# Opening stage of a hybrid decoder layer: inverse root by Ln and Exp, conditioning loads issued three k tiles ahead, two squares added before their sum

## Chip, cores and metric

One core of a Trainium2 chip runs the whole program. The metric is the device time in microseconds (us), the median of several executions. Engines: PE is TensorE (matmuls; PEld its weight loads), DVE is VectorE, ACT is ScalarE, POOL is GpSimd, SP is the sync engine, which issues nearly all DMAs here.

## The reference, cut to what matters

One decoder layer on a sequence of 1024 tokens of width 1024. The change touches only its opening: RMSNorm of x, scaled and shifted by a conditioning vector, and the first columns of the input projection.

```python
c_act = jax.nn.silu(c)
shift, scale, gate = jnp.split(c_act @ ada_w + ada_b, 3, axis=-1)
h = rms_norm(x, norm_g) * (1 + scale[:, None, :]) + shift[:, None, :]
(sq, sk, sv, sz, dq, dk_, dv_, dz, ...) = jnp.split(h @ w_in, offsets, axis=-1)
...   # three token mixers (stick-breaking attention, gated DeltaNet, GLA)
merged = g_sb * (y_sb @ proj_sb) + g_gdn * (y_gdn @ proj_gdn) + g_gla * (y_gla @ proj_gla)
return x + gate[:, None, :] * (merged @ w_out)
```

`rms_norm` is x · 1/sqrt(mean(x²) + 1e-6) · g, with the mean over the 1024 channels of a token.

## The kernel before

The activations lie transposed, channels on the 128 partitions: eight k tiles `xs[k]` of 128 channels by 1024 tokens. Every projection needs h in two parts, `h_hi` (rounded for fast matmuls) and `h_lo` (the remainder), so a product is three matmuls of 128x512 where one would do.

**Order of work.** PE's instructions run in the order in which the program text makes them. On all other engines and in SP's queue a planner reorders: it goes by the order of the text, by its own forecast of when inputs are ready, and it gives out the buffers of one tag in the order of the text. Each queue then runs strictly in the planned order, and waits where an input or a buffer is late.

**The sum of squares (lines 311 to 333).** `square` makes x² of a k tile on POOL, DVE or ACT. `add_up` has PE multiply by a matrix of ones into two PSUM banks, one for each half of the tokens; a float32 matmul of 128x512 is two passes in the trace, so one `add_up` is four passes. There are five: k tiles 0, 1, 2 alone, then 3+4+5 added up, then 6+7. The inverse root is ACT's Sqrt of each half and DVE's reciprocal of each half (line 333). A dummy Sqrt (line 322) is there to have the table of that function loaded early.

**The conditioning (lines 341 to 369).** Each k tile needs two columns of `mod`, shift and scale. For k tiles 0 and 1 `by_product` has PE do it, two tiles of `ada` with 16 matmuls of one column (32 records) each pair. For k tiles 2 to 7 `by_rows` has DVE do it: two loads of 512 KB (line 352) and two reductions over 128x1024 (line 367). The tiles come from the pool `hp` (tag "h", 16 buffers), which also holds the 16 tiles of h.

**The k loop (lines 377 to 420).** For k tile k: `by_rows`; `split` of the raw weights (ACT line 151, DVE line 152); `amp` (line 398); x·amp·rstd on DVE (line 403), `h_hi` on ACT (line 406), `h_lo` on DVE (line 408); then 24 matmuls of 128x512 on PE into eight PSUM banks, in the order h_hi, h_lo, h_hi. The raw weights (line 381 for k up to 2, line 392 for later ones) have three buffers. In the text the ada loads of k tile k (k from 3) stand at the head of its own turn, after the h tiles of the k tiles before it.

**What follows.** The small projections, then head 1's projections as filler between the DeltaNet steps. Eight more reductions of the same kind, for the later `gate` (lines 297 to 301), stand much further down in the text; the planner fits them in where it sees DVE free.

Of the kernel before, what the change touches and what calls it, by code (L numbers as in the profile page):

```python
# [15 lines left out]
AF = mybir.ActivationFunctionType  # L16
# [3 lines left out]
P = 128  # L20
D = 1024
T = 1024
KT = D // P
# [10 lines left out]
O_DQ, O_DK, O_DV, O_DZ = 2048, 2560, 3072, 3584  # L34
# [18 lines left out]
def kernel(ctx: ExitStack, tc: tile.TileContext, xT: bass.AP, c: bass.AP,  # L53
# [3 lines left out]
    nc = tc.nc  # L57
# [15 lines left out]
    def big(tag, w=1024, dt=F32):  # L73
        return mp.tile([P, w], dt, tag=tag, name=tag, bufs=3 if tag == "u5" else 2)
# [4 lines left out]
    def bank(pool, tag, *shape):  # L79
        return pool.tile([P, *shape], F32, tag=tag, name=tag)  # L80
# [12 lines left out]
    def mm(out, lhsT, rhs, cost, **kw):  # L93
        clock[0] += cost
        return nc.tensor.matmul(out, lhsT=lhsT, rhs=rhs, **kw)  # L95
# [17 lines left out]
    def C(name, i=0, n=1):  # L113
        o = COLS[name][0] + i
        return col[:, o:o + n]
# [14 lines left out]
    one_c = ones[:, 0:1]  # L130
    eps_c = cp.tile([P, 1], F32, name="eps_c")
# [9 lines left out]
    c_row = big("u8")  # L141
    for hf in range(2):
        sl = slice(hf * HALF, (hf + 1) * HALF)
# [5 lines left out]
    def split(hi, lo, raw, scale=None):  # L149
        if scale is None:  # L150
            nc.scalar.copy(out=hi, in_=raw)  # L151
            nc.vector.tensor_sub(out=lo, in0=raw, in1=hi.bitcast(F32))  # L152
        else:
            nc.scalar.activation(out=hi, in_=raw, func=AF.Copy, scale=scale)  # L154
            nc.vector.scalar_tensor_tensor(out=lo, in0=raw, scalar=scale, in1=hi.bitcast(F32),  # L155
                                           op0=ALU.mult, op1=ALU.subtract)

    def raw_tile():
        return wp.tile([P, 4, P], F32, tag="raw", name="raw")
# [144 lines left out]
    ms = [bank(pl, "lv", HALF) for _ in range(2)]  # L304
    halves = [slice(hf * HALF, (hf + 1) * HALF) for hf in range(2)]
    root = cp.tile([P, 1], F32, name="root")

    def square(k, out, eng):
        for sl in halves if k == KT - 1 else (slice(0, T),):
            if eng is nc.scalar:  # L310
                eng.activation(out=out[:, sl], in_=xs[k][:, sl], func=AF.Square)
            else:
                eng.tensor_mul(out=out[:, sl], in0=xs[k][:, sl], in1=xs[k][:, sl])
        return out

    def add_up(x2, start=False, stop=False):
        for hf, sl in enumerate(halves):
            mm(ms[hf], ones, x2[:, sl], 858, start=start, stop=stop)

    for k, eng in ((0, nc.gpsimd), (1, nc.vector), (2, nc.scalar)):  # L320
        add_up(square(k, big(("u4", "u4", "u5")[k]), eng), start=(k == 0))
    nc.scalar.activation(out=root, in_=one_c, func=AF.Sqrt)
    part, more = square(3, big("u6"), nc.vector), [big("u6"), big("u5")]
    for k in (4, 5):
        nc.vector.tensor_add(out=part, in0=part, in1=square(k, more[k - 4], nc.scalar))
# [2 lines left out]
    rstd = big("u5")  # L328
    for hf, sl in enumerate(halves):
        nc.vector.tensor_add(out=last[0][:, sl], in0=last[0][:, sl], in1=last[1][:, sl])  # L330
        mm(ms[hf], ones, last[0][:, sl], 858, start=False, stop=True)
        nc.scalar.activation(out=rstd[:, sl], in_=ms[hf], func=AF.Sqrt, scale=1.0 / D, bias=eps_c)
        nc.vector.reciprocal(out=rstd[:, sl], in_=rstd[:, sl])
    na = cp.tile([P, 1], F32, name="na")
    amp = cp.tile([P, KT], F32, name="amp")


    PRE = 2
    first_mod = bank(pt, "tr", HALF)

    def both(ap, k):
# [2 lines left out]
    def conditioning2(k):  # L344
        tiles = [hp.tile([P, T], F32, tag="h", name="ada") for _ in range(2)]
        if k < PRE:
            for i, t in enumerate(tiles):
                nc.sync.dma_start(out=t, in_=adaP[2 * k + i])
            return lambda: by_product(k, tiles)
        for i, t in enumerate(tiles):  # L350
            j = 8 * i + k
            nc.sync.dma_start(out=t, in_=adaT[j * P:(j + 1) * P, :])
        return lambda: by_rows(k, tiles)

    def by_product(k, tiles):
        for i, t in enumerate(tiles):
            at = 2 * k + i
            for kk in range(KT):
                mm(first_mod[:, at:at + 1], t[:, kk * P:(kk + 1) * P], c_col[:, kk:kk + 1], 120,
                   start=(kk == 0), stop=(kk == KT - 1))  # L360
        nc.vector.tensor_add(out=both(mod, k), in0=first_mod[:, 2 * k:2 * k + 2],
                             in1=both(C("ada_b", 0, 24), k))

    def by_rows(k, tiles):
        for i, t in enumerate(tiles):
            j = 8 * i + k
            nc.vector.tensor_tensor_reduce(out=t, in0=t, in1=c_row, scale=1.0, scalar=0.0,
                                           op0=ALU.mult, op1=ALU.add, accum_out=mod[:, j:j + 1])
        nc.vector.tensor_add(out=both(mod, k), in0=both(mod, k), in1=both(C("ada_b", 0, 24), k))
# [3 lines left out]
    f_ps = [[None, None] for _ in first]  # L373
    f_banks = ((pa, "acc"), (pa, "acc"), (pm, "mx"), (pm, "mx"), (pt, "tr"), (pl, "lv"),
               (pl, "lv"), (pl, "lv"))
    raws, conds = [], []
    for k in range(KT):
        conds.append(conditioning2(k))
        raw = raw_tile()
        wsrc = w_in[k * P:(k + 1) * P, O_DQ:O_DQ + 4 * 512].rearrange("p (g n) -> p g n", g=4)  # L380
        nc.sync.dma_start(out=raw, in_=wsrc[:, :, 0:P])
        raws.append(raw)
        if k == 2:
            break
    for k in range(PRE):
        conds[k]()
    for k in range(KT):
        if k >= 3:
            conds.append(conditioning2(k))
            raw = raw_tile()  # L390
            wsrc = w_in[k * P:(k + 1) * P, O_DQ:O_DQ + 4 * 512].rearrange("p (g n) -> p g n", g=4)
            nc.sync.dma_start(out=raw, in_=wsrc[:, :, 0:P])
            raws.append(raw)
        if k >= PRE:
            conds[k]()
        w = wp.tile([P, 2, 4, P], F32R, tag="w", name="w")
        split(w[:, 0], w[:, 1], raws[k])
        nc.vector.scalar_tensor_tensor(out=amp[:, k:k + 1], in0=mod[:, 8 + k:9 + k], scalar=1.0,
                                       in1=C("norm_g", k), op0=ALU.add, op1=ALU.mult)
        hi = hp.tile([P, T], F32R, tag="h", name="h_hi")  # L400
        lo = hp.tile([P, T], F32R, tag="h", name="h_lo")
        for sl in halves if k == 0 else (slice(0, T),):
            nc.vector.scalar_tensor_tensor(out=xs[k][:, sl], in0=xs[k][:, sl],
                                           scalar=amp[:, k:k + 1], in1=rstd[:, sl],
                                           op0=ALU.mult, op1=ALU.mult)
            nc.scalar.activation(out=hi[:, sl], in_=xs[k][:, sl], func=AF.Identity,  # L406
                                 bias=mod[:, k:k + 1])
            nc.vector.scalar_tensor_tensor(out=lo[:, sl], in0=xs[k][:, sl],  # L408
                                           scalar=mod[:, k:k + 1],
                                           in1=hi[:, sl].bitcast(F32),  # L410
                                           op0=ALU.add, op1=ALU.subtract)
        h_hi.append(hi)
        h_lo.append(lo)
        for g in range(4):
            for hf in range(2):
                if k == 0:
                    pool, tag = f_banks[2 * g + hf]
                    f_ps[g][hf] = bank(pool, tag, HALF)
                sl = slice(hf * HALF, (hf + 1) * HALF)
                for n, (a, r) in enumerate(((0, hi), (0, lo), (1, hi))):  # L420
                    mm(f_ps[g][hf], w[:, a, g, :], r[:, sl], 216,
                       start=(k == 0 and n == 0), stop=(k == KT - 1 and n == 2))
# [53 lines left out]
    raw = big("u7").rearrange("p (k n) -> p k n", k=KT)  # L476
    for o, dst, n in ((O_LR, 0, RANK), (O_DB, 32, NH), (O_DA, 64, NH)):
        nc.sync.dma_start(out=raw[:, :, dst:dst + n],
                          in_=w_in[:, o:o + n].rearrange("(k p) n -> p k n", p=P))
# [858 lines left out]
    for n, (h, q) in enumerate(halves):  # L1338
        g, key = G[h], f"{h}.{q}"
# [9 lines left out]
    for n, (h, q) in enumerate(halves):  # L1349
        g, key = L[h], f"{h}.{q}"  # L1350
# [80 lines left out]
```

## Time and profile before

| | us |
|---|---|
| median of 3 runs | 1532.16 |
| lowest and highest run | 1530.81 and 1535.56 |
| the profiled execution | 1534.0 |
| its span | 1532.2 |
| PE busy in the span | 1480.8 (97%) |
| DVE busy | 851.6 (56%) |
| ACT busy | 676.5 (44%) |
| idle of PE before lines waiting on h_hi and h_lo of the k loop | 13.9 and 5.8 |

Busy time of PE is not PE at its peak: the granted clock has two levels, 2.4 GHz (1.00 in the profile) and 1.2 GHz (0.50), and a matmul at the lower one counts as busy for twice as long. The idle time in front of a group of instructions is put down to what ended it. Over the whole span PE is nearly always busy; the views of the first 110 us are what this case is about.

### The profile page before, as it was taken

What the parts mean: (1) busy time and instruction counts of PE and PEld (TensorE: products, weight loads), DVE (VectorE), ACT (ScalarE), POOL (GpSimd) and SP (SyncE); (2) the same over time, 40 slices, a digit from 0 to 9 for tenths busy, and PEclk for the clock granted to TensorE, in tenths of its full rate; (3) what the DMA queues carried; (4) which work ended last, traced back from release to release, by engine and by line L of the source; (5) the groups of instructions that cost most, each with busy time, mean ns of one, the idle gap of its engine ahead of it and who ended that gap; (6) DMA issues with size and microseconds to landing.
All of it is one profiled execution on the core that took longest, in us unless ns stands there. A gap on an engine that the chain in (4) does not pass through costs nothing.

```text
span 1532.2 us, 26643 instructions
## 1 busy us (share of the span) xinstructions
PE 1480.8 (97%) x10632; PEld 1241.6 (81%) x10632; DVE 851.6 (56%) x1839; ACT 676.5 (44%) x1468; POOL 148.6 (10%) x295
## 2 busy tenths in 40 slices
PE   8779999999999999999999999999999999999998
PEld 5658777777878787878878999899988888888887
DVE  5776746656653566757666524553555326474721
ACT  5136846452563646647466623342434442322200
POOL 1001223224230000000000100010000000000000
PEclk7889999999999999999999999999999999999999
DMA  7532423131232111112121212110222334353342
GB/s 253 199 97 55 112 75 88 50 91 43 64 93 71 42 43 52 46 53 60 49 60 29 77 56 62 49 36 27 58 69 83 106 107 124 118 148 117 119 144 76
DMA packets 162470, 126.48 MB, mean 83 GB/s; under 512 B 23429, under 2 KB 139269, under 8 KB 162346
## 3 DMA queue, kind: packets, MB, share of 16 engines
q1 hardware_dynamic: 162202, 124.47, 27.6%
q8 instruction: 83, 1.36, 0.4%
q14 instruction: 41, 0.34, 0.1%
q10 hardware_dynamic: 144, 0.31, 0.1%
HBM read 99.80 MB, written 24.95 MB: 81 GB/s over the span
## 4 chain that ended last, share of the span: by engine, by line
PE 80%; DVE 9%; ACT 3%; issue 3%; DMA 3%; POOL 2%; SPq 0%; POOLq 0%; DVEq 0%; ACTq 0%
PE acc L95 64%; PE lv L95 6%; PE mx L95 6%; PE tr L122 2%; DVE u L431 2%; PE tr L95 1%; DVE w L152 1%; DVE w L616 1%; DVE w L618 1%; POOL c L284 1%; DMA v<-gam_d 1%; DMA raw<-in_w_in 1%; DVE u L1156 0%; DMA xd<-w 0%; POOL w L642 0%
## 5 line engine op out<-in xcount | busy, mean ns | idle before, releaser
L95 PE MATMUL acc<-h_hi,w 128*128 128x512 f32 x1856 | 658.9, 410 | 13.9 <-ACT h_hi L406 13.9
L95 PEld LDWEIGHTS acc<-h_hi,w 128*128 128x128 f32 x1856 | 353.0, 190 | 85.9 <-ACT h_hi L406 16.1
L95 PE MATMUL acc<-h_lo,w 128*128 128x512 f32 x928 | 367.4, 396 | 5.8 <-DVE h_lo L408 5.8
L95 PEld LDWEIGHTS acc<-h_lo,w 128*128 128x128 f32 x928 | 177.1, 191 | 35.6 <-DVE h_lo L408 8.8
L95 PE MATMUL acc<-whi,h_hi 128*128 128x256 f32 x640 | 186.9, 292 | 0.0
L95 PE MATMUL acc<-wlo,h_hi 128*128 128x256 f32 x640 | 180.7, 282 | 0.0
L95 PE MATMUL acc<-whi,h_lo 128*128 128x256 f32 x640 | 180.7, 282 | 0.0
L95 PE MATMUL acc<-u,w 128*128 128x512 f32 x768 | 176.5, 391 | 0.0
L95 PEld LDWEIGHTS acc<-u,w 128*128 128x128 f32 x768 | 144.2, 188 | 31.6
L151 ACT CAST w<-raw 128x512 fp32r<-128x512 f32 x144 | 84.9, 619 | 149.8 <-PE acc L95 90.3
L152 DVE TENSOR_TENSOR w<-raw,w 128x512 fp32r<-128x512 f32 x144 | 97.5, 688 | 56.5 <-ACT w L151 55.8
L95 PEld LDWEIGHTS acc<-whi,h_hi 128*128 128x128 f32 x640 | 122.3, 191 | 1.4 <-issue 0.7
L95 PEld LDWEIGHTS acc<-wlo,h_hi 128*128 128x128 f32 x640 | 122.4, 191 | 0.1
L95 PEld LDWEIGHTS acc<-whi,h_lo 128*128 128x128 f32 x640 | 122.2, 191 | 0.0
L284 POOL TENSOR_TENSOR c<-c,mhalf 128x4 f32<-128x4 f32 (+1 forms) x56 | 55.0, 981 | 582.3 <-DVE c L282 580.9
L95 PE MATMUL acc<-m_hi,w 128*128 128x512 f32 x256 | 79.0, 389 | 0.0
L1156 DVE TENSOR_TENSOR_SCAN u<-u,zero_c 128x128 f32<-128x128 f32 (+7 forms) x32 | 43.4, 1356 | 36.3 <-ACT u L1154 36.3
L155 DVE SCALAR_TENSOR_TENSOR w<-raw,col,w 128x128 fp32r<-128x128 f32 x96 | 29.5, 349 | 55.3 <-ACT w L154 55.3
L95 PEld LDWEIGHTS mx<-r,u 128*128 128x128 f32 x288 | 44.1, 190 | 17.3 <-DVE r L797 4.9
L95 PEld LDWEIGHTS acc<-m_hi,w 128*128 128x128 f32 x256 | 48.0, 188 | 10.0
L95 PE MATMUL mx<-r,u 128*128 128x128 f32 x288 | 48.4, 280 | 5.6 <-POOL u L766 2.2
L95 PE MATMUL lv<-u,u 128*32 128x32 f32 (+5 forms) x528 | 48.9, 250 | 4.0 <-DVE u L699 4.0
(256 smaller groups left out, 2169.1 us busy)
## 6 DMA issues: line engine op xcount, KB each, us to landing
raw<-in_w_in SPq DMA_DIRECT2D x160, 256.0 KB, 3.0
g_dram<-v SPq DMA_DIRECT2D x36, 256.0 KB, 2.2
v<-g_dram SPq DMA_DIRECT2D x36, 256.0 KB, 2.7
u<-in_xT SPq DMA_DIRECT2D x16, 512.0 KB, 5.0
u<-y_dram SPq DMA_DIRECT2D x16, 512.0 KB, 3.7
ada<-in_adaT SPq DMA_DIRECT2D x12, 512.0 KB, 4.5
u<-in_adaT SPq DMA_DIRECT2D x8, 512.0 KB, 4.0
v<-gam_d SPq DMA_DIRECT2D x16, 256.0 KB, 3.3
```

Source lines behind the costliest of these rows:

```text
L95: return nc.tensor.matmul(out, lhsT=lhsT, rhs=rhs, **kw)
L122: nc.tensor.transpose(out=out, in_=in_, identity=ident[:k, :k])
L151: nc.scalar.copy(out=hi, in_=raw)
L152: nc.vector.tensor_sub(out=lo, in0=raw, in1=hi.bitcast(F32))
L155: nc.vector.scalar_tensor_tensor(out=lo, in0=raw, scalar=scale, in1=hi.bitcast(F32), op0=ALU.mult, op1=ALU.subtract)
L284: nc.gpsimd.tensor_tensor(out=out, in0=out, in1=mhalf[:, 0:n], op=ALU.pow)
L431: nc.vector.scalar_tensor_tensor(out=t, in0=r[:, tap:tap + T], scalar=C("conv", j + tap), in1=t, op0=ALU.mult, op1=ALU.add)
L616: nc.vector.tensor_tensor(out=t3, in0=L3[:, w:16, j:w].broadcast_to([32, n, w]), in1=Xl3[:, j:w, 0:w].broadcast_to([32, n, w]), op=ALU.mult)
L618: nc.vector.tensor_sub(out=Xl3[:, w:16, 0:w], in0=Xl3[:, w:16, 0:w], in1=t3)
L1156: nc.vector.tensor_tensor_scan(om[:, 0:n][:, ::-1], om[:, 0:n][:, ::-1], zero_c.broadcast_to([P, n]), 1.0, ALU.mult, ALU.add)
```

## The change

Four edits, all in the opening.

- The squares of k tiles 1 and 2 are added on DVE and go through one `add_up`, and the one of k tile 0 follows: four `add_up`s in place of five.
- The inverse root is Ln of each half on ACT, then one Exp with scale -0.5 over all 1024 tokens. The two reciprocals are gone. The dummy is a Square and an Ln on an element of `c_row`, so that it comes after the Silu that makes `c_row`.
- The loads of k tiles 3 to 7 are asked for three turns earlier: at turn k, behind the h pair of k tile k, first the raw weights and then the ada pair of k tile k+3.
- The order of the first three turns' loads is as it was.

```diff
-    for k, eng in ((0, nc.gpsimd), (1, nc.vector), (2, nc.scalar)):
-        add_up(square(k, big(("u4", "u4", "u5")[k]), eng), start=(k == 0))
-    nc.scalar.activation(out=root, in_=one_c, func=AF.Sqrt)
+    low = [square(k, big(("u4", "u4", "u5")[k]), eng)
+           for k, eng in ((0, nc.gpsimd), (1, nc.vector), (2, nc.scalar))]
+    nc.vector.tensor_add(out=low[1], in0=low[1], in1=low[2])
+    add_up(low[1], start=True)
+    add_up(low[0])
+    nc.scalar.activation(out=root, in_=c_row[:, T - 1:T], func=AF.Square)
+    nc.scalar.activation(out=root, in_=root, func=AF.Ln, bias=one_c)
...
-        nc.scalar.activation(out=rstd[:, sl], in_=ms[hf], func=AF.Sqrt, scale=1.0 / D, bias=eps_c)
-        nc.vector.reciprocal(out=rstd[:, sl], in_=rstd[:, sl])
+        nc.scalar.activation(out=rstd[:, sl], in_=ms[hf], func=AF.Ln, scale=1.0 / D, bias=eps_c)
+    nc.scalar.activation(out=rstd, in_=rstd, func=AF.Exp, scale=-0.5)
...
-    for k in range(KT):
-        conds.append(conditioning2(k))
-        raw = raw_tile()
...
+    AHEAD = 3
...
+    def load_first(k):
         raw = raw_tile()
         wsrc = w_in[k * P:(k + 1) * P, O_DQ:O_DQ + 4 * 512].rearrange("p (g n) -> p g n", g=4)
         nc.sync.dma_start(out=raw, in_=wsrc[:, :, 0:P])
+        return raw
+
+    for k in range(AHEAD):
+        conds.append(conditioning2(k))
+        if k < 3:
+            raws.append(load_first(k))
     for k in range(PRE):
         conds[k]()
     for k in range(KT):
-        if k >= 3:
-            conds.append(conditioning2(k))
...
         if k >= PRE:
             conds[k]()
...
+        if k + 3 < KT:
+            raws.append(load_first(k + 3))
+        if k + AHEAD < KT:
+            conds.append(conditioning2(k + AHEAD))
...
```

## Rows read from the trace of the kernel before

**Rows 1.** Stretches: length, busy PE, PEld, DVE, ACT, POOL, PEclk, DMA share, GB/s

```profile
32.27:42.17 9.90, 9.29 (x24) 6.60 (x25) 9.90 (x17) 2.23 (x3) 0.20 (x2) 0.61 0.31 85
42.17:53.30 11.13, 11.04 (x49) 8.82 (x47) 8.25 (x15) 2.31 (x4) 0.00 (x0) 1.00 0.71 236
64.05:77.30 13.25, 8.41 (x24) 6.05 (x24) 10.09 (x18) 1.76 (x2) 0.00 (x0) 0.74 0.52 178
42.17:108.48 66.31, 49.55 (x170) 37.28 (x168) 45.42 (x78) 14.30 (x21) 2.33 (x2) 0.85 0.51 164
108.48:160.00 51.52, 51.52 (x244) 42.89 (x243) 36.61 (x60) 37.12 (x67) 12.35 (x15) 1.00 0.24 62
```

**Rows 2.** What PE waited for from 43 to 108.5: us, times, longest

```profile
PE acc L95 <- ACT h_hi L406: 11.6, 5, 4.2
PE acc L95 <- DVE h_lo L408: 5.2, 5, 1.5
```

**Rows 3.** The chain of waits, 42 to 109: start, us, what

```profile
79.69 5.64 DMA ada<-in_adaT
```

**Rows 4.** SP's queue in order of time: start, us, line, what it issues

```profile
14.43 1.61 SPq L352 DMA_DIRECT2D ada<-in_adaT  x2
...
43.80 0.39 SPq L392 DMA_DIRECT2D raw<-in_w_in  x1
44.23 0.97 SPq L352 DMA_DIRECT2D ada<-in_adaT  x2
```

**Rows 5.** DVE by group, 22 to 108.5: count, busy us, mean ns, idle before

```profile
L367 DVE CUSTOM_DVE_ANT_0 ada<-ada,u 128x1024 f32<-128x1024 f32 x12 | 14.5, 1221 | 3.1 <-DMA ada<-in_adaT 3.0
L299 DVE CUSTOM_DVE_ANT_0 u<-u,u 128x1024 f32<-128x1024 f32 x8 | 9.8, 1219 | 4.6 <-DMA u<-in_adaT 4.6
L403 DVE SCALAR_TENSOR_TENSOR u<-u,amp,u 128x1024 f32<-128x1024 f32 x7 | 9.0, 1281 | 0.2
L408 DVE SCALAR_TENSOR_TENSOR h_lo<-u,mod,h_hi 128x1024 fp32r<-128x1024 f32 x7 | 9.0, 1280 | 0.6 <-ACT h_hi L406 0.6
L152 DVE TENSOR_TENSOR w<-raw,w 128x512 fp32r<-128x512 f32 x10 | 6.8, 689 | 7.8 <-ACT w L151 7.8
...
L398 DVE SCALAR_TENSOR_TENSOR amp<-mod,col 128x1 f32<-128x1 f32 x8 | 1.2, 156 | 0.2
```

**Rows 6.** PE and PEld in order of time, start of the program

```profile
7.88 11.40 PE L95 MATMUL lv<-u,ones 128*128 128x512 f32 x20 [0.38 <-POOL u L313]
...
9.75 0.34 PEld L95 LDWEIGHTS lv<-u,ones 128*128 128x128 f32 x1 [0.52 <-issue]
...
13.81 0.19 PEld L95 LDWEIGHTS lv<-u,ones 128*128 128x128 f32 x1 [0.24 <-issue]
...
19.12 3.63 PE L95 MATMUL tr<-c_col,ada 128*128 128x1 f32 x32
...
23.00 6.99 PE L95 MATMUL tr<-c_col,ada 128*128 128x1 f32 x32 [0.25 <-DVE mod L361]
```

**Rows 7.** DVE in order of time, start of the program

```profile
10.60 1.22 DVE L313 TENSOR_TENSOR u<-u 128x1024 f32<-128x1024 f32 x1 [1.31 <-DMA u<-in_xT]
12.97 2.56 DVE L325 TENSOR_TENSOR u<-u,u 128x1024 f32<-128x1024 f32 x2 [1.15 <-ACT u L311]
...
23.06 6.56 DVE L333 RECIPROCAL u<-u 128x512 f32<-128x512 f32 x2
...
30.71 1.41 DVE L403 SCALAR_TENSOR_TENSOR u<-u,amp,u 128x512 f32<-128x512 f32 x2
```

**Rows 8.** ACT in order of time, start of the program

```profile
9.33 1.06 ACT L311 ACTIVATE u<-u 128x1024 f32<-128x1024 f32 x1 [1.19 <-DMA u<-in_xT]
...
19.32 0.69 ACT L332 ACTIVATE u<-lv,eps_c 128x512 f32<-128x512 f32 x1 [0.17 <-PE lv L95]
```

**Rows 9.** ACT later on: an Ln and the next Exp, in order of time

```profile
510.16 0.72 ACT L903 ACTIVATE v<-v,ones 128x512 f32<-128x512 f32 x1
...
515.80 1.28 ACT L944 ACT_TABLE_LOAD   x1
```

More of the change, by code (lines that the diff above doesn't have):

```diff
@@ L375 @@
                (pl, "lv"), (pl, "lv"))
-    raws, conds = [], []
-    for k in range(KT):
-        conds.append(conditioning2(k))
+    def load_first(k):
         raw = raw_tile()
@@ L381 @@
         nc.sync.dma_start(out=raw, in_=wsrc[:, :, 0:P])
-        raws.append(raw)
-        if k == 2:
-            break
+        return raw
+    raws, conds = [], []
+    for k in range(AHEAD):
+        conds.append(conditioning2(k))
+        if k < 3:
+            raws.append(load_first(k))
     for k in range(PRE):
@@ L387 @@
     for k in range(KT):
-        if k >= 3:
-            conds.append(conditioning2(k))
-            raw = raw_tile()
-            wsrc = w_in[k * P:(k + 1) * P, O_DQ:O_DQ + 4 * 512].rearrange("p (g n) -> p g n", g=4)
-            nc.sync.dma_start(out=raw, in_=wsrc[:, :, 0:P])
-            raws.append(raw)
         if k >= PRE:
```

## The prediction

> **What bounds the kernel now.** Over the whole span PE is nearly always busy, so a microsecond saved matters where PE stands still or runs at its lower level. I read the stretches first [rows 1]. From 42.17 to 108.48, k tiles 1 to 7 of the opening loop, PE is busy for 49.55 of 66.31 us and the granted clock averages 0.85. Two k tiles in the middle of it, 42.17 to 53.30, show what dense work looks like: 11.04 us busy for 48 matmuls at clock 1.00, so 5.5 us a k tile. A later one, 64.05 to 77.30, takes 13.25 us at clock 0.74: some 5 us of idle, and 8.41 us of busy time for work worth 5.5. Seven dense k tiles would need 7 x 5.5 = 38.5 us; the stretch is 66.31 - 38.5 = 27.8 us longer. Next, what PE waits for there [rows 2]: h_hi 11.6 us and h_lo 5.2, which is all of its 16.8 us of idle. The other 11 us are the lower level after each gap.
>
> Then what makes h late. The chain of waits goes through the landing of an ada pair, 5.64 us at 79.69 [rows 3]. SP's queue says why it is late [rows 4]: the pair of k tile 2 is issued at 14.43, that of k tile 3 only at 44.23, behind a raw load at 43.80. Nothing but its place holds it there. The pool has 16 buffers, six hold ada tiles, and the text asks for k tile 3's pair behind three h pairs. DVE's groups tell the same from the other side [rows 5]: reductions idle 3.0 us for ada, the later gate's reductions, squeezed between, 4.6 us for theirs, and the weight split 7.8 us for ACT. DVE is busy for 45.42 of the 66.31 us [rows 1], so it isn't full.
>
> **The change part by part.**
>
> *Squares.* One DVE add of 1.28 us (two took 2.56) [rows 7] replaces one `add_up`. PE's passes fall from 20 to 16. But PE now begins with the sum of squares 1 and 2. ACT's square of k tile 2 ends at 9.33 + 1.06 = 10.4 [rows 8]; the new dummy adds a table load of 1.28 us after the Silu, half of which falls into ACT's 1.19 us of waiting, so 10.4 to 10.9. With the add: 11.7 to 12.2. If DVE squares k tile 3 first (10.60 to 11.82) it is 13.1 [rows 7]. PE thus starts at 12.2 (11.7 to 13.1) instead of 7.88 [rows 6]. A weight load with its gap came every 0.86 us at 9.75 and every 0.43 us at 13.81 [rows 6]: the two levels. Before, about five of the 11.4 us lay at the lower one. I take five again: 6 passes at 0.86, 10 at 0.43, 9.5 us in all, so the sum ends at 21.7 where it ended at 19.1. Bounds: 11.7 with only three slow passes gives 19.9, 13.1 with sixteen gives 26.9. So this edit costs 2.6 us (0.8 to 7.8). Counting passes alone would have said a gain of 4 x 0.43 = 1.7. The Trainium skill (TensorE: Matmul & The Clock Gate, The HAM clock gate) says that the throttled state is the default and that activity releases it. By that rule taking early work from PE delays its rise; the rows of the 20 passes agree, 0.86 before 0.43.
>
> *by_product.* Its 32 records took 3.63 us at the upper and 6.99 us at the lower level [rows 6]. [...] The first may lose the upper, since the sum ends later; I take 5 us. So mod of k tile 0 is there at 26.7, and the second ends at 26.7 + 0.3 + 7.0 = 34.0 (bounds 19.9 + 2 x 3.63 = 27.2 and 26.9 + 14.3 = 41.2).
>
> *Inverse root.* Two reciprocals of 3.28 us ran until 29.62, and behind them the first x·amp·rstd only at 30.71 [rows 7]. In their place: Ln of the second half 0.69 (as Sqrt at 19.32) [rows 8], a table load 1.28, Exp about 1.1. That the load is needed shows later in this trace: an Ln at 510.16 and, before the next Exp, a load of 1.28 us at 515.80 [rows 9]. rstd is ready at 21.7 + 0.9 + 1.28 + 1.1 = 25.0, before mod at 26.7, so the root leaves the path. DVE then makes h of k tile 0 at 27 to 30 while PE still runs the second by_product, and PE's 2.3 us of waiting at k tile 0 disappear. What is late next is the second by_product itself. k tile 0 runs from 34.0; with half its 24 matmuls at the lower level that is 12 x 0.46 + 12 x 0.23 = 8.3 us, so to 42.3. Before it ran from 32.27 to 42.17 at clock 0.61 [rows 1]. The start therefore comes out even (5 us better, 7 worse).
>
> *Conditioning loads.* Issued behind the h pair of k, the pair of k+3 has about two and a half turns, some 14 us, where landing took 5.64 [rows 3]. Cover gone, 5.64 us a k tile would come back. In front of it on SP stands the raw load of k+3, which waits until the split of k has freed its buffer; that is before h_lo of k, so it doesn't hold the pair up. Behind them the gate loads wait, which are wanted only at the very end. Buffers: k tile 5's pair needs those of k tile 0, free when by_product is over; k tile 7's those of k tile 4. The wait for ada is gone; what is next is DVE's own work. A k tile costs it two reductions 2.44, 1.28 + 1.28, 0.69 and two small operations of 0.16 [rows 5], 6.0 us; without reductions 3.4. From 34.0 (mod of k tile 1; k tile 2's reductions fit in before): 2 x 3.4 + 5 x 6.0 = 36.8, so h_lo of k tile 7 at 70.8. Eight gate reductions at 1.22 + 0.16 add up to 11.0 and run in this stretch now. None inside: 70.8; all inside: 81.8. Half: 76.3. With the last k tile's 5.5 us the loop ends at 76.3, 81.8 or 87.3 by DVE; by PE, 42.3 + 38.5 = 80.8. I take 82. Before: 108.5. Gain 26.5 us.
>
> *What follows.* From 108.48 to 160 PE never waits, and DVE is busy for 36.61 of 51.52 us [rows 1]. Gate reductions pushed out there, four of them 5.5 us, find 15 us of idle, but the chain of waits runs along DVE there. I charge 3.5 us (0 to 6).
>
> **Sum.** 26.5 - 3.5 = 23 us off. The profiled execution took 1534.0 us, 1.8 above the median, which gives 1511 for it; for the median, 1532.16 - 23 = 1509.
>
> **Rivals.**
>
> A, DVE takes the place of the loads. If the planner keeps one gate reduction in each k tile, DVE needs 6.0 + 1.4 = 7.4 us where PE needs 5.5. PE then waits about 2 us each time, and the lower level comes back, as in the row of clock 0.74, where 24 matmuls took 8.41 busy us [rows 1]. Half of that loss back on each of seven k tiles is 1.5 us: 7 x (7.4 + 1.5) = 62, loop end 104, gain 4.5; where the lower level returns in half of them only, 57, loop end 99, gain 9.5. With nothing given back later, the time is 1523 to 1528. Against it: the gate reductions filled DVE's idle time, which is going.
>
> B, the pairs don't come earlier: the planner gives them the same place on SP, behind raw loads whose buffers are late. Then only the start moves, which comes out even: 1530 to 1534. Against it: the second use of the pool's buffers is what held them, and the text now asks three turns earlier.
>
> C, slower: the late sum. If PE stays at the lower level through all sixteen passes and both by_products, k tile 0 starts at 41.2 instead of 32.27, less the 2.3 us no longer waited: up to 7 us more. It decides only where the loop gains less than that, that is where DVE paces k tiles 1 to 7 at 8.5 us or more. Time 1535 to 1539. For it: the passes at 0.86. Against it: DVE's 6.0.
>
> **How the numbers follow.** Main forecast 0.75: loop end 76 to 87 by the number of gate reductions inside, 5 us better or 7 worse by the start, 0 to 6 us given back; taken together, since the ends hardly meet, 1497 to 1521. A 0.13, B 0.06, C 0.06. The range goes to 1525, into A's times, and leaves out the rest of A, B and C, some 0.18. Differences of 0.3% (4.6 us) are about what a measurement of this kernel can tell from no change. Faster by more: the main case and most of A, 0.86; within: 0.08 (B, the rest of A); slower: 0.06.
>
> **What would show it.** After: the sum of squares with 16 passes starting near 12 and ending near 22; no reciprocal, an Exp ending before mod of k tile 0; ada pairs of k tiles 3 and 4 issued by 40; no DVE idle on ada; PE granted 1.00 through k tiles 1 to 7, each about 5.5 to 6 us; the loop's end near 82. Wrong if PE still waits more than 1 us for h_hi at several k tiles, if the small projections' start doesn't move by 20 us, or if PE waits that are new appear between 80 and 180.

## The result, and the profile after

The changed kernel took 1508.49 us (median of four runs, 1507.0 to 1512.01) against 1533.86 for the kernel before on the same chip: a ratio of 0.9838, interval 0.9809 to 0.9866, so 25 us less where 23 were forecast. The profiled execution took 1507.8 us with a span of 1506.0; before it was 1534.0 and 1532.2. All times of the trace below are from that execution.

First the stretches that answer to [rows 1]: start, length, busy PE, PEld, DVE, ACT, POOL, PEclk, DMA share, GB/s.

```profile
24.66:40.03 15.37, 13.35 (x57) 11.47 (x57) 11.67 (x22) 3.72 (x6) 0.20 (x2) 0.67 0.55 174
40.03:78.11 38.08, 38.08 (x170) 31.54 (x168) 35.95 (x61) 14.82 (x22) 1.82 (x1) 1.00 0.61 185
```

The second line is k tiles 1 to 7. They now take 38.08 us with PE busy all through at clock 1.00; in [rows 1] the same seven took 66.31 us, busy for 49.55 of them at clock 0.85. Both parts of the loss went together: the 16.8 us of idle and the 11 us of lower level behind it. DVE is busy for 35.95 of the 38.08 us, so there is little room left on it.

What PE waits for from 25 to 110, answering to [rows 2] (us, times, longest):

```profile
PE acc L95 <- DVE h_lo L409: 1.8, 1, 1.8
PE tr L95 <- DVE mod L366: 0.3, 1, 0.3
```

The wait for h_hi is gone; the one for h_lo that is left lies in k tile 0. SP's queue, answering to [rows 4], gives the reason: the pairs of k tiles 3 to 7 are issued from 27.04 on instead of 44.23 (the last at 53.98 instead of 84.21), the first of them right behind a raw load.

```profile
26.62 0.38 SPq L384 DMA_DIRECT2D raw<-in_w_in  x1
27.04 0.98 SPq L357 DMA_DIRECT2D ada<-in_adaT  x2
...
34.69 1.58 SPq L357 DMA_DIRECT2D ada<-in_adaT  x2
...
43.15 0.92 SPq L357 DMA_DIRECT2D ada<-in_adaT  x2
...
47.26 0.89 SPq L357 DMA_DIRECT2D ada<-in_adaT  x2
...
53.98 0.98 SPq L357 DMA_DIRECT2D ada<-in_adaT  x2
```

The raw loads of k tiles 3 to 7 are no such cause, though the change asks for them earlier too. Before, the planner had them in the queue ahead of the pairs, two at 30.82, then at 38.23, 43.80 and 49.23:

```profile
30.82 2.31 SPq L392 DMA_DIRECT2D raw<-in_w_in  x2
...
38.23 0.39 SPq L392 DMA_DIRECT2D raw<-in_w_in  x1
...
49.23 0.38 SPq L392 DMA_DIRECT2D raw<-in_w_in  x1
```

After, they go out at 26.62, 34.27, 37.16, 42.66 and 48.25. The last three come 1 us earlier, while the pairs come 17 to 32 us earlier. (The raw load at 43.80 in [rows 4] is that of k tile 6, not of k tile 3.)

DVE by group from 22 to 78.1 (count, busy us, mean ns, idle before), answering to [rows 5]: the reductions (line 372 now) wait for no ada tile, the weight split (line 152) not for ACT, and of the later gate's eight reductions (line 299) two lie in the loop instead of all eight.

```profile
L372 DVE CUSTOM_DVE_ANT_0 ada<-ada,u 128x1024 f32<-128x1024 f32 x12 | 14.5, 1219 | 0.0
...
L152 DVE TENSOR_TENSOR w<-raw,w 128x512 fp32r<-128x512 f32 x10 | 6.8, 687 | 0.0
...
L299 DVE CUSTOM_DVE_ANT_0 u<-u,u 128x1024 f32<-128x1024 f32 x2 | 2.4, 1215 | 1.9 <-DMA u<-in_adaT 1.9
```

PE at the start, answering to [rows 6] (start, us, instruction, in brackets the idle time before it and what ended it):

```profile
12.05 9.11 PE L95 MATMUL lv<-u,ones 128*128 128x512 f32 x16 [4.36 <-DVE u L322]
20.99 3.63 PE L95 MATMUL tr<-c_col,ada 128*128 128x1 f32 x32
24.88 5.72 PE L95 MATMUL tr<-c_col,ada 128*128 128x1 f32 x32 [0.25 <-DVE mod L366]
30.46 0.77 PE L95 MATMUL acc<-h_hi,w 128*128 128x512 f32 x1
33.03 0.79 PE L95 MATMUL acc<-h_lo,w 128*128 128x512 f32 x1 [1.80 <-DVE h_lo L409]
```

The sum of squares begins when DVE's add (line 322) is done and has 16 passes. ACT at the start, answering to [rows 8], shows the new root: two Ln, a table load of 1.28 us, one Exp, done at 24.25.

```profile
20.34 0.69 ACT L336 ACTIVATE u<-lv,eps_c 128x512 f32<-128x512 f32 x1 [3.11 <-PE lv L95]
21.20 0.69 ACT L336 ACTIVATE u<-lv,eps_c 128x512 f32<-128x512 f32 x1 [0.17 <-PE lv L95]
21.90 1.28 ACT L337 ACT_TABLE_LOAD   x1
23.19 1.06 ACT L337 ACTIVATE u<-u 128x1024 f32<-128x1024 f32 x1
```

And a wait that the kernel before doesn't have, from the waits of PE from 78 to 130:

```profile
PE tr L122 <- DVE gam_c L541: 4.0, 1, 4.0
```

**The ledger.** The loop ends at 78.1 instead of 108.5, 30.4 us earlier. By the end of the DeltaNet preparation's triangular solve (PE's last wait for DVE's u there) 175.24 stands against 201.72, 26.5 us earlier, and at the end of the span 26.2. So 3.9 of the 30.4 us go in the 97 us behind the loop, and almost nothing after that. The stretch from the loop's end to that point, before and after, with the columns of [rows 1]:

```profile
108.48:201.72 93.24, 86.85 (x523) 70.92 (x522) 67.06 (x176) 68.40 (x121) 23.91 (x42) 0.98 0.31 78
```

```profile
78.11:175.24 97.13, 89.77 (x523) 72.65 (x522) 75.41 (x194) 70.32 (x122) 26.58 (x43) 0.95 0.38 102
```

PE does the same work (523 records of matmuls in both) and stands idle for 7.4 us instead of 6.4: the new wait of 4.0 us makes it late, and it then waits 3.3 us inside the solve where before it waited 6.4. The larger part, 2.9 us, is busy time: the granted clock averages 0.95 instead of 0.98. From the start of the new wait on, 112.83 to 125.16, it is 0.72; before, the same work (142.94 to 155.70) ran at 1.00.

### The profile page after: what moved, and what is told of

The parts are those of the page before. It is cut to its first block, busy times and chain, and to the rows that moved or that the text cites. A ratio compares the mean times of both kernels' runs of the same rounds, so it can differ in the third digit from the quotient of the medians.

```text
span 1506.0 us, 26643 instructions
## 1 busy us (share of the span) xinstructions
PE 1467.5 (97%) x10628; PEld 1235.0 (82%) x10628; DVE 844.5 (56%) x1838; ACT 679.5 (45%) x1471; POOL 150.5 (10%) x295
## 4 chain that ended last, share of the span: by engine, by line
PE 83%; DVE 8%; ACT 3%; DMA 3%; POOL 2%; issue 2%; SPq 0%; POOLq 0%; DVEq 0%; ACTq 0%
PE acc L95 66%; PE lv L95 7%; PE mx L95 6%; PE tr L122 2%; DVE u L436 1%; PE tr L95 1%; DVE w L621 1%; DVE w L623 1%; DVE w L152 1%; POOL w L647 1%; POOL c L284 1%; DMA w<-ad 1%; DMA w<-xd 1%; DVE u L1161 1%; DMA u<-in_xT 0%
## 5 line engine op out<-in xcount | busy, mean ns | idle before, releaser
L155 DVE SCALAR_TENSOR_TENSOR w<-raw,col,w 128x128 fp32r<-128x128 f32 x96 | 29.5, 349 | 55.7 <-ACT w L154 48.9
L95 PE MATMUL lv<-u,u 128*32 128x32 f32 (+5 forms) x528 | 48.9, 251 | 2.6 <-DVE u L704 2.6
```

## The experiments

Each was measured against the kernel before on the same chip; that kernel's medians were 1534.2, 1534.5 and 1534.8 us in the three groups. "Loop end" is PE's end with the 24 matmuls of k tile 7 in the profiled execution. The changed kernel itself was measured in the first and the third group, not in the second, which has the kernels with pairs two ahead, without gate reductions and with the low part first; comparisons of these with it go across groups, which are on different chips. Expectations name the changed kernel, the one before and the theories as they stood then.

### Which edit carries the gain

**The changed kernel again**, for its scatter.

> The changed kernel again, beside the parts of it that follow, so that they can be compared with it on one chip. Both theories expect 24 to 26 us less than before (ratio 0.983 to 0.985).

Measured: 1511.86 us, ratio 0.9852 (0.9837 to 0.9866). Loop end at 81.8 instead of 78.1, and the new wait of 4.0 us is there again. The instructions are the same; PE's first 40 us aren't:

```profile
11.68 10.13 PE L95 MATMUL lv<-u,ones 128*128 128x512 f32 x16 [4.03 <-DVE u L322]
21.65 4.15 PE L95 MATMUL tr<-c_col,ada 128*128 128x1 f32 x32
26.05 6.99 PE L95 MATMUL tr<-c_col,ada 128*128 128x1 f32 x32 [0.25 <-DVE mod L366]
32.90 0.77 PE L95 MATMUL acc<-h_hi,w 128*128 128x512 f32 x1
```

Here the second small product runs at the lower level to its end (6.99 us against 5.72), and k tile 0 with it: from 30 to 42 the granted clock is 0.51. A loop end thus carries 4 us of scatter from one execution to the next.

**The loads alone**, with root and squares as before:

```diff
+    AHEAD = 3
...
-        if k >= 3:
-            conds.append(conditioning2(k))
...
+        if k + 3 < KT:
+            raws.append(load_first(k + 3))
+        if k + AHEAD < KT:
+            conds.append(conditioning2(k + AHEAD))
```

> The loads three turns ahead alone; root and squares as before. Theory (the loads are the gain): the sum of squares ends at 19.1 us and k tile 0 starts near 32.3 as before, k tiles 1 to 7 run on PE's time (38 us, no wait above 1 us), so the loop ends near 81 instead of 108.5, and 3 to 5 us are given back later: 22 to 25 us less, ratio 0.984 to 0.986. Rival (DVE's reciprocals were the brake, the loads merely follow): less than 8 us, ratio above 0.995, and h_hi still waits at several k tiles.

Measured: 1510.77 us, ratio 0.9848 (0.9834 to 0.9862), the same as the changed kernel beside it. Loop end at 81.4. PE's waits from 25 to 110:

```profile
PE acc L95 <- ACT h_hi L403: 2.3, 1, 2.3
PE acc L95 <- DVE h_lo L405: 0.6, 2, 0.4
```

All of it lies in k tile 0; k tiles 1 to 7 run without a wait though the reciprocals are still there. Within the intervals the loads are the whole gain. The run moves raw weights and ada pairs together; that it is the pairs is read from SP's queue above, and no run moves one of the two alone by three turns.

**The root alone**, with loads and squares as before:

```diff
...
-        nc.scalar.activation(out=rstd[:, sl], in_=ms[hf], func=AF.Sqrt, scale=1.0 / D, bias=eps_c)
-        nc.vector.reciprocal(out=rstd[:, sl], in_=rstd[:, sl])
+        nc.scalar.activation(out=rstd[:, sl], in_=ms[hf], func=AF.Ln, scale=1.0 / D, bias=eps_c)
+    nc.scalar.activation(out=rstd, in_=rstd, func=AF.Exp, scale=-0.5)
```

The dummy is that of the changed kernel as well.

> Logarithm and exponential alone; loads and squares as before. Theory (the loads are the gain): k tile 0 starts at 30 instead of 32.3, and the waits for the ada pairs of k tiles 3 to 7 stay, so the loop ends 0 to 4 us earlier: ratio 0.997 to 1.000. Rival (6.6 us of DVE's reciprocals were the brake): 15 us or more, ratio below 0.990.

Measured: 1534.58 us, ratio 1.0004 (0.9991 to 1.0016). k tile 0 starts at 29.82 instead of 32.27, and the loop ends at 108.1 instead of 108.5. PE's waits from 25 to 110:

```profile
PE acc L95 <- ACT h_hi L407: 11.6, 5, 4.6
PE acc L95 <- DVE h_lo L409: 8.0, 6, 1.8
```

Of these, 1.8 us of h_lo lie in k tile 0. k tiles 1 to 7 begin at 39.67 instead of 42.17 and take 68.43 us instead of 66.31: PE is idle for 17.8 us instead of 16.8, and busy for 50.64 instead of 49.55, at clock 0.83 instead of 0.85. DVE's reductions idle 10.0 us for ada pairs there, where [rows 5] has 3.0. So most of an earlier start is waited away in the loop, and the root alone is worth nothing.

**The squares alone**, with loads and root as before:

```diff
-    for k, eng in ((0, nc.gpsimd), (1, nc.vector), (2, nc.scalar)):
-        add_up(square(k, big(("u4", "u4", "u5")[k]), eng), start=(k == 0))
...
+    nc.vector.tensor_add(out=low[1], in0=low[1], in1=low[2])
+    add_up(low[1], start=True)
+    add_up(low[0])
```

> The squares of k tiles 1 and 2 added up, alone; root and loads as before. Theory (a late start of the sum costs time at PE's lower level): the sum starts near 12 instead of 8 and ends 1.5 to 3 us later than before, k tile 0 starts 1 to 3 us later, the loop ends 0 to 3 us later: ratio 1.000 to 1.002. Rival (four passes fewer): 1.7 us earlier, ratio 0.999.

Measured: 1534.61 us, ratio 1.0003 (0.999 to 1.0017). The sum starts at 11.26 and ends 1.0 us later than in [rows 6]; k tile 0 starts at 32.71, only 0.4 us later, and the loop ends at 107.7, 0.8 us earlier where 0 to 3 us later were expected. In time it is nothing; in this kernel too DVE's reductions idle for ada pairs (3.3 us).

**The changed kernel with five sums**, the squares edit undone:

```diff
...
-    nc.vector.tensor_add(out=low[1], in0=low[1], in1=low[2])
-    add_up(low[1], start=True)
-    add_up(low[0])
+    for k, eng in ((0, nc.gpsimd), (1, nc.vector), (2, nc.scalar)):
+        add_up(square(k, big(("u4", "u4", "u5")[k]), eng), start=(k == 0))
```

> The changed kernel with the squares as before: k tiles 0, 1 and 2 go through PE each by itself, five sums. Theory (what counts is when PE can begin, and that it has left its lower level by then): the sum starts at 7.9 and ends at 19.1 instead of 21.0, the second product ends at 29 to 30 instead of 30.5, the loop ends 0.5 to 2 us earlier than in the changed kernel. Rival (fewer passes are less time): the sum ends 1.7 us later than in the changed kernel, and so does the loop.

Measured: 1506.58 us, ratio 0.9825 (0.9809 to 0.9841); the changed kernel in the same group had 0.9852. The sum starts at 7.76 and ends at 19.4, k tile 0 starts at 28.58, and the loop ends at 76.3. That is 1.5 to 5.5 us ahead of the three loop ends of the changed kernel (77.8, 78.1, 81.8). With the loads in place the start does pass through to the loop's end: from the first matmul of k tile 0 to there it is 47.6 to 48.9 us in the changed kernel (three times), in the loads alone and here, for starts between 28.58 and 33.35. By the medians the squares edit looks like a cost of 2 to 5 us; but the intervals of the two ratios overlap, and a later pair of kernels turns it round (below).

### What the loads are worth, and what they cost elsewhere

**Ada pairs two tiles ahead**, raw weights still three:

```diff
-        if k + AHEAD < KT:
-            conds.append(conditioning2(k + AHEAD))
+        if 3 <= k + 2 < KT:
+            conds.append(conditioning2(k + 2))
```

> The changed kernel with the ada pairs asked for two turns ahead instead of three (the first three pairs and the raw weights as in the changed kernel). Theory (the pair's place in the order decides, and a turn and a half of some 8 us is longer than the 5.6 us to landing): PE waits at most 1 us at a k tile, the loop ends 0 to 4 us later than in the changed kernel (82 to 86), ratio to before 0.984 to 0.988. Rival (the queue's own waits eat the lead, so that only three turns are enough): half of the gain is lost, ratio 0.991 to 0.994.

Measured: 1514.06 us, ratio 0.9859 (0.9838 to 0.988). Pairs are issued at 37.16, 45.34, 51.30, 57.57 and 63.93, DVE idles 0.8 us for them, five gate reductions fall into the loop, and PE waits 5.1 us in all for h_lo, 3.3 of them in k tiles 1 to 7. Loop end at 85.7. Most of the gain is there as soon as the pair doesn't stand at the head of its own turn; the third turn of lead is worth some 4 to 8 us of loop end, and what it buys there is hardly the landing any more (0.8 us of idle), but, as the five gate reductions suggest, less of DVE's time in the loop; this is argued from one trace. k tile 0 starts at 32.93 here; the execution of the changed kernel with the same start (32.90) ends the loop at 81.8, which makes it 4 us.

**The kernel before without the gate reductions**, as a check on what they cost there:

```diff
+    nc.vector.memset(mod[:, 16:24], 1.0)
...
-        for j in range(16, 24):
-            conditioning(j, "u6", "u5")
```

> The kernel before without the eight later gate reductions and their loads; the gate columns of mod are set to 1, so this part is left out. It tells whether the gate reductions inside the loop were the brake, and the change helped only by driving them out. Theory (the ada pairs' place was the brake): PE still waits for h_hi and h_lo over 12 us in all in the loop, the loop ends at 104 to 109, the time is 0 to 4 us less than before. Rival (eight reductions of 1.4 us were the brake): the loop ends at 97 or earlier and the time falls by 11 us or more, ratio below 0.993.

Measured: 1529.52 us, ratio 0.9968 (0.9953 to 0.9984); loop end at 103.7. DVE's reductions for the k tiles there, from 43 to the loop's end:

```profile
L368 DVE CUSTOM_DVE_ANT_0 ada<-ada,u 128x1024 f32<-128x1024 f32 x10 | 12.1, 1223 | 9.8 <-DMA ada<-in_adaT 9.8
```

The reductions' idle for ada grows from 3.0 us [rows 5] to 9.8: what DVE saved became waiting for the pairs. Most of what the gate reductions took had only filled the gap. They cost the old loop 5 us, a little more than the 0 to 4 us expected; the loads' place cost it some 23 (the gain of the loads alone).

**The changed kernel without the gate reductions**, by the same edit, for the new wait of 4.0 us:

> The changed kernel without the eight later gate reductions and their loads; the gate columns of mod are set to 1, so this part of the computation is left out. Theory (the microseconds given back behind the loop come from reductions that DVE now runs there): PE's wait of 4.0 us for the copy of the transposed gates falls below 2.8 us, since one reduction of 1.26 us stands right before that copy, and the time is 2 to 4 us under the changed kernel. Rival (the chain of the small projections is as long as it is and the loop's end now comes before it is through): the wait stays at 3 us or more and the time is within 1 us.

Measured: 1507.42 us, ratio 0.982 (0.9796 to 0.9845), 1 to 4 us under the three medians of the changed kernel, which is within their scatter. Loop end at 81.0; the wait on gam_c is gone, and the solve's last wait ends 94.9 us behind the loop, where it was 97.1 with the reductions and 93.2 in the kernel before. So the reductions make the new wait, and 2.2 of the 3.9 us given back by there. Of the new wait's 4.0 us and the lower level behind it, the solve gives some back: its own waits are 6.3 us again without the reductions, as before the change (6.4), and 3.3 with them. The other 1.7 us are PE's level once more:

```profile
80.95:175.84 94.89, 88.50 (x524) 71.96 (x522) 68.22 (x176) 68.53 (x121) 23.05 (x42) 0.96 0.29 76
```

Idle time is 6.4 us here as in the kernel before, and busy time 88.50 against 86.85. The difference lies in the solve, where PE is granted 0.78 (from 160) against 0.88 in the kernel before, in one execution each. Why the level falls further there is not settled.

**Gate reductions held back until the gates are made**, on top of two repairs of the next section:

```diff
...
+        with tc.issue_after(gate_last[0].ins):
+            for j in range(16, 24):
+                conditioning(j, "u6", "u5")
```

> As the kernel with both repairs, and the eight gate reductions queued on DVE behind the copies of the transposed gates. Theory (the reductions in front of those copies make PE wait 4.0 us there): that wait falls under 0.5 us. What then counts is the triangular solve behind it: if the reductions stand in its way there, PE waits longer at the first matmul after it (now some 3 us) and the time stays within 1 us of the kernel with both repairs; if they fit into DVE's gaps, it is 2 to 4 us less.

Measured: 1513.03 us, ratio 0.9862 (0.9841 to 0.9883), 4 us slower than the same kernel without the hold, where no change or a gain was expected. The wait on gam_c is gone and a longer one is there:

```profile
PE tr L122 <- DVE u L589: 17.2, 1, 17.2
```

The eight reductions now stand between 118.31 and 139.6 in DVE's order, in front of the product of line 589, which PE's transposes need. The same eight reductions cost more there: their place on DVE counts, not only their number.

### The wait that was not foreseen

**Low part of k tile 0 first.** In the changed kernel PE waits 1.80 us at 33.03 for h_lo of k tile 0. DVE's order there shows why:

```profile
26.51 0.75 DVE L404 SCALAR_TENSOR_TENSOR u<-u,amp,u 128x512 f32<-128x512 f32 x1
30.63 0.16 DVE L366 TENSOR_TENSOR mod<-tr,col 128x2 f32<-128x2 f32 x1 [3.38 <-PE tr L95]
30.83 0.16 DVE L399 SCALAR_TENSOR_TENSOR amp<-mod,col 128x1 f32<-128x1 f32 x1
31.03 1.29 DVE L404 SCALAR_TENSOR_TENSOR u<-u,amp,u 128x1024 f32<-128x1024 f32 x1
32.23 1.41 DVE L409 SCALAR_TENSOR_TENSOR h_lo<-u,mod,h_hi 128x512 fp32r<-128x512 f32 x2
```

DVE is idle for 3.38 us in front of mod of k tile 1, then makes k tile 1's x·amp·rstd, and only then h_lo of k tile 0, whose inputs (h_hi at 26.74 and 28.0 on ACT) had long been there. The planner had put the small add of k tile 1 first. The edit puts it behind:

```diff
...
-    for k in range(PRE):
-        conds[k]()
+    conds[0]()
+    add_bias(0)
+    conds[1]()
     for k in range(KT):
...
+        if k == 1:
+            with tc.issue_after(h_last[0].ins):
+                add_bias(1)
```

> The changed kernel, with the add of the second product's bias on DVE put behind the two h_lo of k tile 0. Theory (the 1.8 us that PE waits for h_lo of k tile 0 come from DVE's order alone): that wait falls under 0.3 us, k tile 0 ends 1 to 2 us earlier and so does the loop; the time is 0.5 to 2 us under the changed kernel. Rival: the wait goes to k tile 1, whose mod is now later on DVE, and the loop's end stays.

Measured: 1504.04 us, ratio 0.9803 (0.9777 to 0.9828), the best time of all, 4 to 8 us under the three medians of the changed kernel (1508.5, 1509.8, 1511.9), where 0.5 to 2 us were expected. Those were taken in other groups, and the interval overlaps two of their three, so the size isn't settled. DVE makes h_lo of k tile 0 at 25.82 and PE waits for nothing from 25 to 108:

```profile
29.45 0.77 PE L95 MATMUL acc<-h_hi,w 128*128 128x512 f32 x1
30.02 0.63 PE L95 MATMUL acc<-h_lo,w 128*128 128x512 f32 x1
```

Loop end at 75.6. From the first matmul of k tile 0 to there it is 46.1 us, where the changed kernel has 47.6 to 48.9: the wait is worth some 1.5 to 3 us, and the rest of the difference in time is not explained. The wait on gam_c is still 4.0 us.

**The changed kernel a third time**, beside the two kernels that follow.

> The changed kernel once more, on the chip of the three that follow, for comparison. 22 to 26 us less than before, ratio 0.983 to 0.986.

Measured: 1509.8 us, ratio 0.984 (0.9818 to 0.9863); loop end at 77.8, k tile 0 waits 1.80 us for h_lo, the wait on gam_c is 4.0.

**Both repairs: five sums and low part first.**

> The changed kernel with five sums as before and with the second product's bias behind h_lo of k tile 0: both of the two repairs that helped singly. If they add up (each moves the loop's end, by some 2 to 5 and by 2 us): the loop ends at 73 to 75 and the time is 4 to 7 us under the changed kernel, ratio to before 0.978 to 0.981. Rival (the chain of the small projections and of the triangular solve behind the loop sets the end from there on): the loop ends as early, but the time is no better than with one of them, 0.980 to 0.983.

Measured: 1508.67 us, ratio 0.9832 (0.9811 to 0.9853). The repairs don't add up: one alone gave 1506.6, the other 1504.0. Its small products took 4.37 and 6.99 us where the kernel with the low part first took 3.63 and 6.07; k tile 0 starts at 30.80, the loop ends at 76.7 (73 to 75 was expected). That explains a microsecond. From 210 on the waits of PE add up to 16.7 us against 16.1 there, another half; the rest of the 4.6 us between the two medians stays unexplained, and with it the sign of the squares edit: five sums looked 5 us better in one pair and 5 us worse in the other, the second of them across two chips.

## Why the prediction was right, step by step

**The loads** were the step that decided, and it held in mechanism and size. Pairs issued from 27.04 on; no idle of DVE for ada; k tiles 1 to 7 in 38.08 us where 7 x 5.5 = 38.5 was worked out from two dense tiles in [rows 1]. The loads alone gave 0.9848, the whole change 0.9852 in the same group. The first pair shows that it was the place in the text: it was issued at 44.23, 37.16 and 27.04 when it was asked for at the head of its own turn, two k tiles ahead and three. Rival B fell with the first line of SP's queue.

**DVE as the next limit** (rival A) came close and didn't decide. The text took half of the eight gate reductions into the loop, and DVE's last h_lo at 76.3 (70.8 to 81.8); two fell in, that h_lo was done at 70.0, DVE was busy for 35.95 of 38.08 us, and PE set the pace. The margin of 1.2 us for this, from 80.8 to 82, wasn't needed. With pairs two ahead five reductions fell in and PE waited 3.3 us: DVE does take the loads' place, as rival A says, but at a lower price: 0.5 to 1.1 us at a k tile instead of 2, and the lower level didn't come back (clock 1.00 from 42 to 85.7).

**The root** did what was said, Exp done at 24.25 (forecast 25.0) and ahead of mod at 24.66, and the load between Ln and Exp that [rows 9] had shown was there. The Trainium skill (ScalarE: Activation LUTs, Table sets: the hidden batching unit) counts one load for ln followed by exp, as one set holds both; this trace shows one for the dummy Ln at 10.84 and another at 21.90. The measurement decides: 1.28 us lie between the second Ln and Exp, as [rows 9] had them.

**The squares and the first by_product.** The sum started at 12.05 (forecast 12.2) and ended near 21 (21.7), a cost of 1.9 us where 2.6 was taken, inside its bounds. The term that was mis-sized is by_product. The text feared that the later sum would take the first product to 5 us and the second to the whole 7.0; they took 3.63 and 5.72, so k tile 0 could begin at 30.46, not 34.0. In the second execution they took 4.15 and 6.99, and k tile 0 began at 32.90, in the third at 29.92: 34.0 lay behind the latest of the three.

**k tile 0.** The text had its h made while PE still runs the second product, and PE's wait gone. That held for h_hi and failed for h_lo. The step named what became late next as the second product alone and overlooked DVE's order, in which h_lo stands behind an instruction that itself waits for that product. PE paid 1.80 us for it, and the kernel with h_lo first doesn't.

**The loop's end** was thus 78.1 against 82: 3.5 us from the earlier start and 1.2 from the margin, 0.4 from k tiles 1 to 7, less 1.3 from a k tile 0 that took 9.6 us, not 8.3.

**What was given back**: forecast 3.5 us (0 to 6), measured 30.4 - 26.2 = 4.2. By the text's own criterion (new waits between 80 and 180) a sign of error appeared, the 4.0 us on gam_c, and it was the charge that the text had made, in a shape that it had not named: not DVE's chain in itself, but PE's wait and the lower level behind it. The size came near, in part by luck, as the charge named no wait. The cause, reductions pushed out of the loop, was right as far as the wait goes: it vanishes when they are left out and when they are held back. It covers 2.2 of the 3.9 us lost by the end of the solve; the other 1.7 stay open. How the reductions make the wait is told in the last section. Together, +3.9 at the loop's end and -0.7 behind it give the 3 us between forecast and profiled execution (26.2 against 23).

**Rival C**, the late sum, had a chance of 0.06 and met the right place: the start does move by several microseconds with PE's level. It could not decide, as k tiles 1 to 7 gained 28.2 us.

## What to carry to other kernels

A tile pool that several streams share hands out its buffers in the order of the text, so a load's place in the text decides when it is issued; look in the queue's rows for loads that are issued late for no reason of data, and compare the landing time with the turns of lead. Before crediting an edit ahead of such a loop, ask what the loop waits for: of the root's 2.4 us of earlier start 0.4 reached the loop's end. And work that filled idle time on DVE has to go somewhere when that idle time goes: the same gate reductions cost a wait of 4.0 us in one place and 17.2 us in another.

## What the runs showed of the hardware

**A small operation on POOL took longer behind a run of DVE operations.** The chain from the loop's end to gam_c goes through an add on POOL of 4x512 (line 498 before, 503 after). Before and after:

```profile
115.95 4.15 POOL L498 TENSOR_SCALAR u<-v,col 4x512 f32<-4x512 f32 x1
121.27 1.56 POOL L498 TENSOR_SCALAR u<-v,col 4x512 f32<-4x512 f32 x1
```

```profile
86.22 7.09 POOL L503 TENSOR_SCALAR u<-v,col 4x512 f32<-4x512 f32 x1
94.06 1.56 POOL L503 TENSOR_SCALAR u<-v,col 4x512 f32<-4x512 f32 x1
```

The second add takes 1.56 us in both, with gaps on DVE beside it (1.56 to 2.55 us over all the traces); the first takes 4.15 and 7.09 us beside a DVE without a gap. DVE after, in that stretch, with a gate reduction (line 299) among its operations:

```profile
85.57 1.63 DVE L436 SCALAR_TENSOR_TENSOR u<-u,col,u 128x1024 f32<-128x1024 f32 x1
87.12 0.67 DVE L152 TENSOR_TENSOR v<-v,v 16x512 fp32r<-16x512 f32 x1
87.73 1.27 DVE L436 SCALAR_TENSOR_TENSOR u<-u,col,u 128x1024 f32<-128x1024 f32 x1
88.92 1.21 DVE L299 CUSTOM_DVE_ANT_0 u<-u,u 128x1024 f32<-128x1024 f32 x1
90.06 0.07 DVE L299 DVE_READ_ACCUMULATOR2_ANT mod<- 128x1 f32 x1
90.06 1.27 DVE L436 SCALAR_TENSOR_TENSOR u<-u,col,u 128x1024 f32<-128x1024 f32 x1
...
91.87 1.08 DVE L152 TENSOR_TENSOR v<-v,v 16x512 fp32r<-16x512 f32 x1
```

The first of POOL's two adds took 7.09 us in all seven profiled executions in which one gate reduction stood in this run of DVE's and the pairs were three ahead (the changed kernel three times, the loads alone, five sums, low part first, both); 7.70 with pairs two ahead, also with a reduction; and 4.15 in the five without one (before, squares alone, the two kernels without gate reductions, the one that holds them back). With the root alone, where DVE's order differs, it took 1.90. DVE is slowed too: at 85.57, beside POOL's copy and the start of its first add, line 436 takes 1.63 us where 1.28 is usual, and at 91.87, some 1.4 us before that add ends, line 152 takes 1.08 us where the same shape took 0.67. The Trainium skill (SBUF — State Buffer, Terms) has the two engines share one pair of ports, held for a whole instruction, with the loser blocked and not merely slowed; these rows agree, with 0.3 to 0.4 us on DVE's side and 5.5 us (7.09 against 1.56) on POOL's. Why the add gets through only behind several operations of DVE, no row shows.

So, with a reduction of 1.21 us in the run, POOL's step was 2.9 us longer, and another one (115.10, right in front of the copies that make gam_c) added 1.3 us (to the end of its small add, 116.44). Counted from the loop's end, gam_c was made at 34.3 us before and at 38.6 after, 4.3 us later, and PE, which reaches its transposes some 34.6 us behind the loop in both, waited 4.0. The two terms are read from the traces of the kernels; that the reductions make the wait is shown by the two kernels that move or remove them. With pairs two ahead the first reduction stands in POOL's way and the second is not in front of the copies: PE's wait there is 2.7 us instead of 4.0, which fits the 1.3 us of the second. It isn't a clean separation, as PE also reaches its transposes later in that kernel, 36.5 us behind the loop's end.

**The same program starts differently.** Three executions of the changed kernel had loop ends of 77.8, 78.1 and 81.8 us. Their sums start within 0.6 us of each other (11.49, 12.05 and 11.68); what differs more is PE's level after that. During the second small product the granted clock was 0.66, 0.63 and 0.50, and in k tile 0 it was 0.66, 0.68 and 0.60. A difference of 4 us at the loop's end, read from one trace each, is no evidence on an edit to the start.
